# Row sums of a 64 MB tensor: eight blocks of 16 rows a partition in place of three blocks of 32, 48 and 48

## The chip, the core and the metric

The kernel runs on one core of one Trainium2 chip. The time is that of one execution on the device, in microseconds (us). Three runs of the kernel before gave a median of 160.50 us (160.49 to 160.85). A further execution was recorded by the hardware profiler; its views are what is read here.

## The reference

The input `x` has 32 x 512 x 1024 float32 values, 16,384 rows of 1,024 values (4 KB a row, 67.1 MB in all). The output is the sum of each row, 16,384 float32 values (64 KB).

```python
def reference(x):                                   # x: (32, 512, 1024) float32
    return np.sum(x, axis=-1).astype(np.float32)    # (32, 512)
```

## The kernel before, in words

The 16,384 rows are spread over the 128 partitions, 128 rows for each (`C = 128`). They are not given out in one go but in blocks. `BLOCKS = (32, 48, 48)` (L10) says how many consecutive rows of a block belong to one partition: in block 0 partition p has rows 32p to 32p+31, in the second block 48 consecutive rows of those that follow, and so on. The function `block` (L28) makes the two views: `x_b`, with one long line of `n` x 1,024 values a partition, and `out_b`, with `n` results a partition. In memory the first row of one partition is therefore `n` x 4 KB from that of the next: 128 KB in block 0, 192 KB in the others.

Work goes by groups of `G = 16` rows a partition (L42), eight groups in all: two in block 0, three in each other block. A group is 128 x 64 KB = 8.39 MB, loaded into one of three buffers `xt0` to `xt2` (L48). Each partition's 64 KB of a group are one contiguous run.

All transfers are issued by SyncE (the queue "SPq" of the profile), in the order of the list `loads` (L90 to L103, issued at L146 to L149). Group 0 comes as one row (semaphore `first`) and then the 15 others; groups 1 to 6 as one load each; the last group as pieces of 9, 4 and 2 rows (`piece0` to `piece2`, from `CUTS`) and its last row as 544 and 480 values (`tail0`, `tail1`). From the fourth group on SyncE waits, ahead of the load, for VectorE to have reduced the group whose buffer is used again (L148). The two first loads are moved ahead of the start-up of the program (L174 to L194).

VectorE reduces whole groups (L109 to L116); in group 6 ScalarE takes 7 of the 16 rows by activations with an accumulated sum (L132 to L135). The pieces of the last group are shared between both (L118 to L123, L137 to L143), and the last row is reduced by VectorE in two halves (L125 to L129). Each block has its own tile of results, `res0` to `res2`, with a column for each row of a partition.

The end is what the second part of the change touches. After the last load SyncE waits for `piece2` and for the sums of all groups but the last (L150 to L152). It then issues three early stores, one for each block (L153 to L155): 32 columns, 48 columns, and the first 32 of the last block's 48. It waits for every sum (L157, L158), stores the last group's 16 columns (L159), waits for the early stores (L161, L162), clears the semaphores (L163) and waits for the last store (L164).

Of the kernel before, what the change touches and what calls it, by code (L numbers as in the profile page):

```python
# [6 lines left out]
COPY = mybir.ActivationFunctionType.Copy  # L7
X = mybir.AxisListType.X

BLOCKS = (32, 48, 48)  # L10
LEAD = 1
G = 16
BUFS = 3
# [6 lines left out]
def row_sums(nc, x: bass.AP, out: bass.AP):  # L20
# [3 lines left out]
    C = R // P  # L24
    assert R % P == 0 and C == sum(BLOCKS) and all(n % G == 0 for n in BLOCKS)
    out_flat = out.rearrange("a (b c) -> (a b c)", c=1)

    def block(r0, n):  # L28
        x_b = x_flat[r0 : r0 + P * n].rearrange("(p c) d -> p (c d)", p=P)
        out_b = out_flat[r0 : r0 + P * n].rearrange("(p c) -> p c", p=P)  # L30
        return x_b, out_b

    def sbuf(name, n):
        return nc.alloc_sbuf_tensor(name, [P, n], F32)

    n_groups = C // G
    groups, stores = [], []
    r0 = 0
    for k, n in enumerate(BLOCKS):
        x_b, out_b = block(r0, n)  # L40
        res = sbuf(f"res{k}", n)
# [8 lines left out]
    pairs = [sbuf(f"pairs{i}", D // 2) for i in range(3)]  # L50

    names = [f"slot{i}" for i in range(BUFS)] + ["first", "piece0", "piece1", "piece2", "tail0"]
    names += ["tail1", "vec", "act", "early0", "early1", "early2", "store"]
    sems = {n: nc.alloc_semaphore(n) for n in names}
    slots = [sems[f"slot{i}"] for i in range(BUFS)]
    vec, act = sems["vec"], sems["act"]
# [76 lines left out]
    _, res, c = groups[b]  # L133
# [12 lines left out]
    for b, dst, src, s in loads:  # L146
        if b >= BUFS:
            nc.sync.wait_ge(vec, freed[b - BUFS])  # L148
        nc.sync.dma_start(out=dst, in_=src).then_inc(s, 16)  # L149
    nc.sync.wait_ge(sems["piece2"], 16)  # L150
    nc.sync.wait_ge(vec, body_vec)
    nc.sync.wait_ge(act, body_act)  # L152
    for k, (out_b, res, n) in enumerate(stores):  # L153
        m = n - G if k == len(stores) - 1 else n
        nc.sync.dma_start(out=out_b[:, 0:m], in_=res[:, 0:m]).then_inc(sems[f"early{k}"], 16)  # L155
    out_z = stores[-1][0]
    nc.sync.wait_ge(vec, count["vec"])  # L157
    nc.sync.wait_ge(act, count["act"])  # L158
    nc.sync.dma_start(out=out_z[:, c_z : c_z + G], in_=res_z[:, c_z : c_z + G]).then_inc(sems["store"], 16)  # L159

    for k in range(len(stores)):  # L161
        nc.sync.wait_ge(sems[f"early{k}"], 16)  # L162
    nc.sync.sem_clear(range(numbers[0], sems["store"].num))  # L163
    nc.sync.wait_ge(sems["store"], 16).then_inc(sems["store"], -16)  # L164
# [2 lines left out]
def kernel(tc: tile.TileContext, x: bass.AP, out: bass.AP):  # L167
    tc.close()
    tc.compile()  # L169
    nc = tc.nc  # L170
    row_sums(nc, x, out)

    sp = mybir.EngineType.SP
    fn = nc.m.functions[0]
    entry, body = None, None
    for blk in fn.blocks:
        ops = [i for i in blk.instructions if i.engine == sp]
        if entry is None:  # L180
            entry = blk
        elif any(i.opcode == "DMACopy" for i in ops):
            body = blk
            break
    code = list(body.instructions)
    loads = [i for i in code if i.engine == sp and i.opcode == "DMACopy"][:EARLY]
    for load in loads:
        assert not load.sync_info.on_wait
        code.remove(load)
    body.instructions = code  # L190
    code = list(entry.instructions)
    at = next(k for k, i in enumerate(code) if i.engine == sp and i.opcode == "Drain")
    code[at:at] = loads
    entry.instructions = code  # L194
# [29 lines left out]
```

## Time and profile before

| what | value |
|---|---|
| median of three runs | 160.50 us |
| the profiled execution's own time | 160.73 us |
| its span, from the first to the last instruction | 159.4 us |
| VectorE (DVE) busy | 121.5 us |
| ScalarE (ACT) busy | 17.2 us |
| bytes read, written | 67.11 MB, 0.07 MB |
| mean rate over the span | 421 GB/s |
| stores from issue to landing | 1.4 to 1.6 us |

How to read the views: DVE is VectorE, ACT ScalarE, SP (or SPq) SyncE. The row of digits has the busy share of the DMA engines in 40 equal slices of the span, in tenths. The chain that ended last is followed back from the last instruction, at each step to what released it. The timeline has start, duration, engine, line and operation, and in brackets how long the engine had been idle and what ended that. A wait is put down to the one that came last. The table by stretches has, for each stretch, its length, the busy time of VectorE, ScalarE and GpSimd with the number of instructions, the granted clock of TensorE, the share of the DMA engines and the rate.

### The profile page before, as it was taken

How to read it: one execution, taken by the hardware profiler on the slowest of the kernel's cores; microseconds unless marked ns; L12 is line 12 of the kernel's file. 1: busy time of each engine (PE TensorE's matmuls, PEld its weight loads, DVE VectorE, ACT ScalarE, POOL GpSimd, SP SyncE). 2: the span in 40 equal slices, each digit the busy share in tenths (PEclk: the TensorE clock that was granted, in tenths of full speed). 3: DMA queues.
4: the chain of work that ended last, by engine and by line, in shares of the span. 5: the costliest groups of instructions: out<-in, count | busy, mean ns of one | idle time of the engine just before them, and what ended most of it. 6: DMA issues, size and time to landing. Idle time of an engine off the chain costs nothing.

```text
span 159.4 us, 110 instructions
## 1 busy us (share of the span) xinstructions
DVE 121.5 (76%) x17; ACT 17.2 (11%) x31; POOL 0.2 (0%) x4
## 2 busy tenths in 40 slices
DVE  1100059994799968999499994999949999499685
ACT  3000000000000000000000000000000000494694
POOL 0000000000000000000000000000000000000000
DMA  9988996996997989969969969969979799699994
GB/s 378 493 370 370 493 526 263 526 526 263 526 477 312 526 378 411 526 263 526 526 263 526 526 263 526 526 263 526 460 329 526 312 477 526 296 444 444 387 400 151
DMA packets 2448, 67.18 MB, mean 421 GB/s; under 512 B 784, under 2 KB 912, under 8 KB 1168
## 3 DMA queue, kind: packets, MB, share of 16 engines
q1 hardware_dynamic: 2448, 67.18, 98.2%
HBM read 67.11 MB, written 0.07 MB: 421 GB/s over the span
## 4 chain that ended last, share of the span: by engine, by line
DMA 75%; DVE 22%; SPq 1%; issue 0%
DMA xt<-in_x_dram 50%; DMA tail<-in_x_dram 25%; DVE res L63 22%; SPq L149 1%; DVE pairs L81 0%; DVE res L81 0%
## 5 line engine op out<-in xcount | busy, mean ns | idle before, releaser
L63 DVE TENSOR_REDUCE res<-xt 128x16 f32<-128x16384 f32 (+5 forms) x10 | 119.9, 11994 | 34.1 <-DMA xt<-in_x_dram 34.1
L74 ACT ACTIVATE xt<-xt 128x1024 f32<-128x1024 f32 x15 | 15.6, 1043 | 138.3 <-DMA xt<-in_x_dram 138.3
L74 ACT ACTIVATION_READ_ACCUMULATOR xt<-xt 128x1 f32 x15 | 2.8, 187 | 0.0
L107 DVE MEMSET tail<- 128x1 f32 x1 | 0.1, 59 | 2.0 <-PEq L169 2.0
L74 ACT ACT_TABLE_LOAD x1 | 1.3, 1283 | 1.9 <-PEq L169 1.9
L81 DVE CUSTOM_DVE_ANT_0 pairs<-tail 128x272 f32<-128x272 f32 (+1 forms) x2 | 0.9, 428 | 0.1
L81 DVE CUSTOM_DVE_ANT_0 pairs<-xt 128x512 f32<-128x512 f32 x1 | 0.7, 693 | 0.2 <-DMA xt<-in_x_dram 0.2
L81 DVE DVE_READ_ACCUMULATOR2_ANT res<- 128x1 f32 x2 | 0.2, 82 | 0.0
L208 POOL MEMSET const-bfloat16-1.0<- 128x1 bf16 x1 | 0.1, 102 | 0.0
L208 POOL MEMSET const-uint8-127<- 128x1 uint8 x1 | 0.1, 101 | 0.0
L208 POOL MEMSET const-float32-0.0<- 128x1 f32 x1 | 0.1, 99 | 0.2 <-issue 0.2
L208 POOL MEMSET const-float32-1.0<- 128x1 f32 x1 | 0.1, 98 | 0.0
L81 DVE DVE_READ_ACCUMULATOR2_ANT tail<- 128x1 f32 x1 | 0.1, 82 | 0.0
## 6 DMA issues: line engine op xcount, KB each, us to landing
xt<-in_x_dram SPq DMA_DIRECT2D x1, 7680.0 KB, 21.2
xt<-in_x_dram SPq DMA_DIRECT2D x1, 4608.0 KB, 32.6
xt<-in_x_dram SPq DMA_DIRECT2D x1, 2048.0 KB, 37.0
xt<-in_x_dram SPq DMA_DIRECT2D x1, 1024.0 KB, 39.0
xt<-in_x_dram SPq DMA_DIRECT2D x1, 512.0 KB, 3.5
tail<-in_x_dram SPq DMA_DIRECT2D x1, 272.0 KB, 39.2
tail<-in_x_dram SPq DMA_DIRECT2D x1, 240.0 KB, 39.3
xt<-in_x_dram SPq DMA_DIRECT2D x6, 40.8
```

The lines of the kernel that those rows point to most:

```text
L63: nc.vector.tensor_reduce(out=res[:, c : c + n], in_=t[:, j * D : (j + n) * D].rearrange("p (j d) -> p j d", d=D), axis=X, op=ADD,).then_i ...
L74: nc.scalar.activation(out=v, in_=v, func=COPY, accum_out=res[:, c + i : c + i + 1]).then_inc(act, 1)
L81: nc.vector.tensor_tensor_reduce(out=pairs[:, 0 : h - a], in0=t[:, a:h], in1=t[:, h:b], scale=1.0, scalar=0.0, op0=ADD, op1=ADD, accum_out ...
L107: nc.vector.memset(tail[:, CUT + 15 : CUT + 16], 0.0).then_inc(vec, 1)
L149: nc.sync.dma_start(out=dst, in_=src).then_inc(s, 16)
L208: nc = _bacc.Bacc("TRN2", target_bir_lowering=False, num_devices=1)
```

## The change

All blocks become 16 rows a partition, so that every block is one group: a partition's 64 KB are followed directly by the next partition's, and a group is 8 MB of `x` without a gap. The groups, their order, their sizes, the buffers, the pieces and the work of VectorE and ScalarE stay. There are eight result tiles of 16 columns instead of three of 32, 48 and 48. The early stores are one for each of the first seven blocks, 16 columns each; the last block has only the last store. They are issued when `piece1` has arrived and no longer when `piece2` has. The semaphores of the early stores are seven instead of three.

```diff
-BLOCKS = (32, 48, 48)
+BLOCKS = (16,) * 8
...
-    names += ["tail1", "vec", "act", "early0", "early1", "early2", "store"]
+    names += ["tail1", "vec", "act"]
+    names += [f"early{k}" for k in range(len(BLOCKS) - 1)] + ["store"]
...
-    nc.sync.wait_ge(sems["piece2"], 16)
+    nc.sync.wait_ge(sems["piece1"], 16)
     nc.sync.wait_ge(vec, body_vec)
     nc.sync.wait_ge(act, body_act)
-    for k, (out_b, res, n) in enumerate(stores):
-        m = n - G if k == len(stores) - 1 else n
-        nc.sync.dma_start(out=out_b[:, 0:m], in_=res[:, 0:m]).then_inc(sems[f"early{k}"], 16)
+    early = stores[:-1]
+    for k, (out_b, res, n) in enumerate(early):
+        nc.sync.dma_start(out=out_b[:, :], in_=res[:, :]).then_inc(sems[f"early{k}"], 16)
     out_z = stores[-1][0]
...
-    for k in range(len(stores)):
+    for k in range(len(early)):
         nc.sync.wait_ge(sems[f"early{k}"], 16)
```

## The prediction

> **What bounds the kernel now.** I read first the page's busy times, slices and queue, to see which resource is never idle.
>
> ```profile
> span 159.4 us, 110 instructions
> DVE 121.5 (76%) x17; ACT 17.2 (11%) x31; POOL 0.2 (0%) x4
> DMA  9988996996997989969969969969979799699994
> q1 hardware_dynamic: 2448, 67.18, 98.2%
> HBM read 67.11 MB, written 0.07 MB: 421 GB/s over the span
> ```
>
> VectorE is busy for 76% of the span, but the one queue that carries all transfers has its packets on the 16 DMA engines for 98.2% of it. The input alone is 67.11 MB. So the kernel is a stream of loads, and everything else matters only at its two ends. The chain that ended last says the same, in order of time (start, length, what):
>
> ```profile
> 1.91 39.07 DMA xt<-in_x_dram
> 41.00 17.23 DVE res L63
> 58.25 40.78 DMA xt<-in_x_dram
> 118.14 39.32 DMA tail<-in_x_dram
> 157.51 0.41 DVE pairs L81
> ```
>
> The VectorE pieces in this chain are not a bound: a reduction of 17.23 us frees a buffer, and the load then issued takes 40.78 us to land because two others lie ahead of it in the queue, which is therefore never empty. What sets the pace is how long one 8.39 MB load takes. I cut the span at the moments when the reductions of successive groups start (length, VectorE busy, ..., GB/s last):
>
> ```profile
> 21.64:41.00 19.36, 16.15 (x1) 0.00 (x0) 0.00 (x0) 1.00 1.00 433
> 41.00:60.36 19.36, 17.23 (x2) 0.00 (x0) 0.00 (x0) 1.00 1.00 433
> 118.42:137.87 19.45, 17.22 (x1) 0.00 (x0) 0.00 (x0) 1.00 0.94 408
> ```
>
> The first is a load from block 0, whose rows a partition lie 128 KB apart from the next partition's (32 rows of 4 KB). The second is from block 1, 192 KB apart. Both take 19.36 us, 433 GB/s with a DMA share of 1.00. The third ran longest, 19.45 us. (Its 408 GB/s counts a shorter stretch of packets; the length is what I use.) Then the end: the timeline, SyncE's own waits, and the stores' times from issue to landing.
>
> ```profile
> 148.88 4.42 DVE L63 TENSOR_REDUCE res<-xt 128x4 f32<-128x4096 f32 x1 [1.25 <-DMA xt<-in_x_dram]
> 153.74 2.29 DVE L63 TENSOR_REDUCE res<-xt 128x2 f32<-128x2048 f32 x1 [0.44 <-DMA xt<-in_x_dram]
> 156.22 1.30 SPq L155 DMA_DIRECT2D out_dram<-res  x3
> 157.84 0.08 DVE L81 DVE_READ_ACCUMULATOR2_ANT res<- 128x1 f32 x1
> 157.95 0.33 SPq L159 DMA_DIRECT2D out_dram<-res  x1
> ```
>
> ```profile
> SPq L155 <- DMA xt<-in_x_dram: 8.5, 1, 8.5
> SPq L164 <- SPq L164: 0.6, 1, 0.6
> SPq L162 <- DMA out_dram<-res: 0.4, 1, 0.4
> SPq L159 <- DVE res L81: 0.3, 1, 0.3
> ```
>
> ```profile
> out_dram<-res SPq DMA_DIRECT2D x2, 16.0 KB, 1.5
> out_dram<-res SPq DMA_DIRECT2D x1, 24.0 KB, 1.6
> out_dram<-res SPq DMA_DIRECT2D x1, 8.0 KB, 1.4
> ```
>
> The reader is to see that SyncE has three early stores out by about 157.6, waits 0.3 us for the last sum (157.92), issues the last store at 157.95, and that this store's landing, 1.4 us later, ends the span at 159.4. The early stores (L162) hold it 0.4 us, inside those 1.4.
>
> **The change, part by part.** The profiled execution took 160.73 us, its span 159.4, so 1.33 us lie around the span; it is 0.23 above the median of 160.50. The terms below are differences, and I put their sum on the median.
>
> *Loads.* The same 13 loads of the same sizes stay, in the same order, on the same queue and in the same buffers; only their addresses move. Each partition's run stays 64 KB, and the next partition's run begins 64 KB further on instead of 128 or 192. Cost from the nearest rows: going from 192 to 128 KB changes the interval by 19.36 - 19.36 = 0.00 us, so I take 0 for going on to 64. Bound from below (a gain): what a perfect layout could remove. The first 0.52 MB load lands at 3.5 us. The trace's packet records start its first packet at 1.0 us, 0.52 MB at 433 GB/s are 1.2, and a semaphore is seen 0.35 us after its packet: 3.5 - 1.0 - 1.2 - 0.35 = 0.95 us lost. The last 16 rows in five loads take 157.46 - 137.87 = 19.59 us against 19.36, 0.23 lost, and the 19.45 us interval adds 0.09. Together 1.27 us; steady loads have nothing to give. Bound from above: the longest interval on all eight groups gives 8 x (19.45 - 19.36) = 0.7 us; the 9-row piece, 148.88 - 137.87 = 11.01 us for 4.72 MB against 10.89 at the steady pace, is 1.1% longer, and 1.1% of the 156 us stream is 1.7 us. So -1.27 to +1.7, and I take 0, from the pitch row, which is the only one that differs in what is changed.
>
> Here the Trainium skill has a rule, "HBM row pitch at large powers of two" (DMA: Bandwidth & Descriptors, section Latency and other measured facts): copies lost rate as the pitch of the rows grew, 207 GB/s at 512 KiB against 214 in full and 103 at 4 MiB, and it advises contiguous tiles or an odd pitch. If its 3% held for the old pitches too, the change would be worth an estimated 4.7 us; the trace does not agree, since 128 KB, a power of two, and 192 KB both run at 433 GB/s, and the sum stays with that row.
>
> *Seven early stores instead of three.* Removed: three issues after the second-last piece of rows (156.22), 1.30 us on SyncE. Added: seven after the piece before it (153.74). The records put the three starts at 156.22, 156.61 and 157.09, and the last end at 157.57, so one store costs SyncE 0.48 us at most. Seven from 153.74 end at 153.74 + 7 x 0.48 = 157.1. SyncE next needs to be free at 157.92, so 0.8 us of cover remain and the cost on the path is 0. SyncE's other two waits before them are over: the last body reduction ended at 147.62, ScalarE's rows at 145.3. Nothing else is queued behind SyncE then; all loads were issued by 118.6. The wait that is dropped, on the 2-row piece, is contained in the later one for the last sum.
>
> *The seven stores on the DMA engines.* They go to the queue behind the last three loads. Their packets: a 64-byte one took 8 to 11 ns and a semaphore 9, so one store is 8 x 10.4 + 9 = 0.09 us on each engine, seven 0.65. The last load's packets end at 157.12. Six stores are waiting by then, the seventh comes about 0.85 us after its issue, at 157.5; all seven are through by about 157.8. The last store's packets ran at 158.78 to 158.99. Cover 0.9 us, cost 0. If all seven went ahead of the last loads instead, it would be +0.65.
>
> *Queue depth.* At 118.6 six loads were unfinished in the queue; now up to eight transfers are. No row shows eight. If only six fit, the last three stores wait for the loads ending at 155.82, 156.50 and 157.12, and the seventh issue ends near 157.6: still under 157.92, cost 0.
>
> *The last store.* 16 columns as before, but its 64-byte pieces now lie next to each other instead of 192 bytes apart. Rows: 1.4 us to landing for it, 1.5 and 1.6 for the early ones, whose pieces also touch. So 0 to +0.2; I take 0, since it is the only 64-byte row and the others were issued back to back.
>
> *Waits at the end.* Seven waits on early stores, not three, and four more numbers in one clearing instruction (51 ns). They run between 158.3 and the landing at 159.36; the early stores have landed by about 158.2. Seven at about 0.05 us are 0.35: hidden, 0.
>
> Sum: 0 + 0 + 0 + 0 + 0 = 0. Time 160.5 us.
>
> The Trainium skill speaks against many small transfers: about 2.0 us fixed for each, mostly overhead under 64 KB (DMA: Bandwidth & Descriptors, Anatomy of one DMA, and Rules for kernel authors). Taken one after the other, four more would be an estimated 8 us; the trace has three in flight at once 0.4 to 0.5 us apart, so this doesn't bear on the sum.
>
> **Rivals.**
> 1. *The new addresses cost the stream time (slower).* All 16 engines now read runs that start at multiples of 64 KB close together; if that loads the memory unevenly, every group takes longer. For it: packets of loads are now and then late (intervals 19.33 to 19.45), so the memory is not wholly out of the picture. Against it: halving-like steps of pitch (192 to 128) cost nothing. Between 0.7 and 1.7 us by the rows above: 161.2 to 162.2. It decides from 0.48 / 8 = 0.06 us an interval on.
> 2. *The early stores get in front of the last loads (slower).* +0.65: 161.2. Against it: the five last loads, queued together at 118, landed strictly in order, which speaks for a queue served in order. It decides only if five of seven pass.
> 3. *The contiguous loads gain at the ends (faster).* Half of the 1.27 us lost at the start and the end: 159.9. For it: the first load runs well under the steady rate. Against it: that may be mere start-up, the same for any address.
> 4. *Nothing of either part reaches the end* is the forecast itself: loads at a rate that addresses don't touch, stores covered.
>
> **How the numbers follow.** About 0.3% of 160.5, 0.48 us, is what can be told from no change. Forecast 0.50 (160.1 to 160.9); rival 1 0.20; rival 2 0.07; rival 3 0.23. So faster 0.23, same 0.50, slower 0.27. The predicted time is the forecast's, 160.5. For 8 in 10 the range goes to 159.7 below (two thirds of what rival 3 could win) and 161.9 above (most of rival 1's span, all of rival 2).
>
> **What would show it.** Right: intervals between group reductions of 19.36 as before, seven store issues on SyncE from 153.7 to about 157, no wait of SyncE on an early store after the last issue, and the last store still issued about 0.03 us after the last sum and landing 1.4 us later. Wrong by rival 1: intervals above 19.42 in every group. Wrong by rival 2: equal intervals up to 118 but the last two loads landing 0.3 to 0.65 us later after the piece that releases the stores. Wrong by rival 3: the first reduction starting before 3.5, or the 19.59 us of the last group shrinking. A landing of the last store over 1.6 us, or an issue of it that waits for SyncE and not for the last sum, would break the zero of the stores.

## The result, and the profile after

The changed kernel takes 161.36 us (median of 6 runs, 161.18 to 161.78), against 160.65 us (160.49 to 160.86) for the kernel before in the same comparison: a ratio of 1.0043, with a 95% interval of 1.0031 to 1.0055. It is slower by 0.7 us. The prediction was 160.5 us with "same" as the likeliest; the measured time is inside its range, but the interval lies above 1. That is a small loss, but one that can be told from no change, and no change was forecast.

The profiled execution of the changed kernel took 161.18 us, the fastest of its six, and the one of before 160.73, so the two traces differ by 0.45 us and not by 0.7. What the slower executions lose beyond that is in neither trace. Line numbers of the changed kernel are one higher (L63 is now L64).

The page of the changed kernel, on the queue:

```profile
q1 hardware_dynamic: 3024, 67.18, 98.2%
```

Still one queue that is full for 98.2% of the span; the 576 additional packets (2448 before) are those of the small stores. The table by stretches of the changed kernel, again cut where the group reductions start (length first, GB/s last):

```profile
22.26:41.61 19.35, 16.15 (x2) 0.00 (x0) 0.00 (x0) 1.00 1.00 434
41.61:60.95 19.34, 17.22 (x1) 0.00 (x0) 0.00 (x0) 1.00 1.00 434
119.01:138.36 19.35, 17.22 (x1) 0.00 (x0) 0.00 (x0) 1.00 0.95 410
```

These are the intervals that took 19.36, 19.36 and 19.45 us before. The pitch is the distance in memory from one partition's run to the next partition's. In this trace the running stream at a pitch of 64 KB is not slower than before. Its start is what differs. Timeline of the changed kernel, VectorE's first two reductions and the last ones, and the stores:

```profile
3.72 1.22 DVE L64 TENSOR_REDUCE res<-xt 128x1 f32<-128x1024 f32 x1 [1.67 <-DMA xt<-in_x_dram]
22.26 16.15 DVE L64 TENSOR_REDUCE res<-xt 128x15 f32<-128x15360 f32 x1 [17.32 <-DMA xt<-in_x_dram]
...
154.17 3.20 SPq L156 DMA_DIRECT2D out_dram<-res  x7
154.18 2.29 DVE L64 TENSOR_REDUCE res<-xt 128x2 f32<-128x2048 f32 x1 [0.45 <-DMA xt<-in_x_dram]
156.66 0.69 DVE L82 CUSTOM_DVE_ANT_0 pairs<-xt 128x512 f32<-128x512 f32 x1 [0.20 <-DMA xt<-in_x_dram]
157.97 0.41 DVE L82 CUSTOM_DVE_ANT_0 pairs<-tail 128x241 f32<-128x241 f32 x1 [0.17 <-DMA tail<-in_x_dram]
158.30 0.08 DVE L82 DVE_READ_ACCUMULATOR2_ANT res<- 128x1 f32 x1
158.41 0.33 SPq L160 DMA_DIRECT2D out_dram<-res  x1
```

The same two first reductions before:

```profile
3.53 1.22 DVE L63 TENSOR_REDUCE res<-xt 128x1 f32<-128x1024 f32 x1 [1.50 <-DMA xt<-in_x_dram]
21.64 16.15 DVE L63 TENSOR_REDUCE res<-xt 128x15 f32<-128x15360 f32 x1 [16.89 <-DMA xt<-in_x_dram]
```

The first reduction starts at 3.72 us (before: 3.53), the second, of the 15 other rows of group 0, at 22.26 (before: 21.64). So 0.62 us are lost by then: 0.19 in the first row, 0.43 in the 15 rows. The 0.19 can't be put down to the pitch: in the traces of this case that start at 128 KB or more, the first row is reduced at anything from 3.48 to 3.90 us. After that nothing more is lost: group 7 starts 0.49 us late (138.36 against 137.87), the last store is issued 0.46 late (158.41 against 157.95) and lands 1.4 us later, as before. SyncE's own waits of the changed kernel:

```profile
SPq L156 <- DMA xt<-in_x_dram: 6.0, 1, 6.0
SPq L160 <- DVE res L82: 0.5, 1, 0.5
SPq L159 <- ACT xt L75: 0.5, 1, 0.5
```

SyncE issues the seven stores in 3.20 us, from 154.17 to 157.37. Until the last store at 158.41 it then waits about 1.0 us, half of it for ScalarE's last row (L159) and half for VectorE's last sum (L160): the stores are covered. The waits for early stores are still there, though none is in this list: the trace has three instructions for them (L163), started at 158.84, 159.01 and 159.18 as early stores land, after 0.10 to 0.14 us of waiting each. The last store lands after that, at 159.82, so they cost nothing, and nor did the 0.4 us before.

### The profile page after: what moved, and what is told of

It reads as the page before. It is cut to its first block, busy times and chain, and to the rows that moved or that the text cites. A ratio compares the mean times of both kernels' runs of the same rounds, so it can differ in the third digit from the quotient of the medians.

```text
span 159.9 us, 116 instructions
## 1 busy us (share of the span) xinstructions
DVE 121.5 (76%) x17; ACT 17.2 (11%) x31; POOL 0.2 (0%) x4
## 3 DMA queue, kind: packets, MB, share of 16 engines
q1 hardware_dynamic: 3024, 67.18, 98.2%
## 4 chain that ended last, share of the span: by engine, by line
DMA 75%; DVE 22%; SPq 1%; issue 0%
DMA xt<-in_x_dram 50%; DMA tail<-in_x_dram 25%; DVE res L64 22%; SPq L150 1%; DVE pairs L82 0%; DVE res L82 0%
## 5 line engine op out<-in xcount | busy, mean ns | idle before, releaser
L64 DVE TENSOR_REDUCE res<-xt 128x16 f32<-128x16384 f32 (+5 forms) x10 | 119.9, 11993 | 34.5 <-DMA xt<-in_x_dram 34.5
```

What stands on the lines that cost most here:

```text
L64: nc.vector.tensor_reduce(out=res[:, c : c + n], in_=t[:, j * D : (j + n) * D].rearrange("p (j d) -> p j d", d=D), axis=X, op=ADD,).then_i ...
```

## The experiments

Run times are medians; times read from a timeline are those of one profiled execution. The kernels come in three sets, each run on a chip of its own together with the kernel before; a ratio is always to the kernel before of the same set. In the code, "..." stands for lines left out.

**The stores alone.** Blocks as before, stores as changed. This and the next three kernels tell apart the loads' addresses and the stores.

```diff
 BLOCKS = (32, 48, 48)
...
-    nc.sync.wait_ge(sems["piece2"], 16)
+    nc.sync.wait_ge(sems["piece1"], 16)
...
-    for k, (out_b, res, n) in enumerate(stores):
-        m = n - G if k == len(stores) - 1 else n
-        nc.sync.dma_start(out=out_b[:, 0:m], in_=res[:, 0:m]).then_inc(sems[f"early{k}"], 16)
+    early = [(o, r, c, c + G) for o, r, n in stores for c in range(0, n, G)][:-1]
+    for k, (out_b, res, i, j) in enumerate(early):
+        nc.sync.dma_start(out=out_b[:, i:j], in_=res[:, i:j]).then_inc(sems[f"early{k}"], 16)
...
```

> Blocks of 32, 48 and 48 rows as before; seven early stores of 16 columns, issued after the 4-row piece. Theory A (the start of the first block at 64 KB costs it all; stores cost nothing): 160.65 us, ratio 1.000, group 0 reduced from about 21.6 us on. Theory B (the seven stores cost the time, through the queue or SyncE): 161.2 to 161.4, with the last store landing or being issued late.

Measured: 160.88 us against 160.86, ratio 0.9998 (0.9987 to 1.0009). Seven early stores, one piece sooner, cost and bring nothing.

**The pitch of the first groups against that of the others.** From the changed kernel, other blocks (one early store for each block or part of it that is not the last group):

```diff
-BLOCKS = (16,) * 8
+BLOCKS = (16, 16, 48, 48)      # the first; the second (32,) + (16,) * 6, the third (48,) + (16,) * 5
...
```

> Blocks of 16, 16, 48 and 48 rows: groups 0 and 1 lie at 64 KB a partition as in the changed kernel, groups 2 to 7 at 192 KB as before; four early stores. Theory A: as slow as the changed kernel, 161.2 to 161.5 us, group 0 reduced from about 22.2 us on. Rival C (the pitch of all eight groups costs a little each, and the late start in the profile was chance): a quarter of the loss, 160.8. Theory B: 160.65 to 160.8.

> Blocks of 32 and then six of 16 rows: groups 0 and 1 lie at 128 KB as before, groups 2 to 7 at 64 KB as in the changed kernel; six early stores. Theory A: no loss, and if the shorter intervals of the changed kernel (19.34 against 19.37 us) belong to the 64 KB pitch, a gain of 0.1 to 0.2: 160.4 to 160.65 us, group 0 from 21.6 us on. Rival C: three quarters of the loss, 161.2. Theory B: 161.2.

> Blocks of 48 and then five of 16 rows: groups 0 to 2 lie at 192 KB, the others at 64 KB; five early stores. Theory A with the reading that only 64 KB is bad at the start: 160.4 to 160.65 us, group 0 from about 21.6 us on. Theory A with the reading that the start worsens with any smaller pitch: earlier than with 128 KB, group 0 from 21.3 us on, 160.2 us. Rival C: 161.1.

Measured, against 160.86: with 16, 16, 48, 48 it is 161.47 us, ratio 1.0033 (1.0023 to 1.0043). With 32 first 160.93, 1.0004 (0.9992 to 1.0016). With 48 first 160.88, 1.0000 (0.9989 to 1.0012). Two groups of 64 KB pitch at the start bring nearly the whole loss; five or six of them later on bring none that can be told. That is Theory A; Theory B and Rival C had 160.8 or less for the first and 161.1 to 161.2 for the others. Its side reading, that the evener intervals at 64 KB are a gain, is not borne out, and nor is a faster start at 192 KB. In the traces group 0 is reduced from 22.51, 22.03 and 21.91 us on. That the second is later than expected lies in its first row (3.90); its 15 rows take 18.13 us after that, as before (18.11).

How the loss arises shows in single packets, which the views only sum up. Each of the 16 engines moves the 15 rows of group 0 in eight packets of 60 KB, one for each of its eight partitions, one after the other. From the packet records of each trace, the mean of 16 packets by turn, in ns (the shortest is 2,265); some of the rows are from kernels that come further on:

```
                                turn 1     2     3     4     5     6     7     8
before             (128 KB)       2316  2293  2280  2268  2269  2269  2268  2269
stores alone       (128 KB)       2275  2268  2269  2268  2269  2269  2267  2268
32 first           (128 KB)       2268  2268  2268  2268  2269  2269  2267  2269
48 first           (192 KB)       2269  2269  2269  2283  2280  2270  2270  2270
64 and 64          (256 KB)       2273  2270  2270  2268  2270  2277  2305  2303
one block          (512 KB)       2441  2356  2268  2268  2271  2270  2267  2269
changed            ( 64 KB)       2333  2318  2366  2416  2287  2268  2267  2267
16, 16, 48, 48     ( 64 KB)       2278  2268  2286  2348  2280  2267  2267  2267
changed, row 15 first (64 KB)     2309  2332  2376  2384  2302  2267  2267  2267
changed, groups swapped (64 KB)   2625  2324  2332  2332  2271  2267  2267  2267
```

At 64 KB the packets of turns 1 to 5, until about 14 us, are long, most of all those of turn 4; from turn 6 on they are at the floor, their shortest time, and in the changed kernel they stay there (the 64 KB packets of groups 1 to 6 have a mean of 2,419 ns with a shortest of 2,418; before the mean was 2,425). Beyond a floor of 2,267 the eight packets cost 0.39 us an engine in the changed kernel and 0.10 before. One reservation: in the profiled execution with 16, 16, 48, 48 the long packets fell on engines that were ahead, and its late start is mostly its first row (4.39 us) and only a little the 15 others:

```profile
4.39 1.22 DVE L64 TENSOR_REDUCE res<-xt 128x1 f32<-128x1024 f32 x1 [2.35 <-DMA xt<-in_x_dram]
22.51 16.15 DVE L64 TENSOR_REDUCE res<-xt 128x15 f32<-128x15360 f32 x1 [16.90 <-DMA xt<-in_x_dram]
```

The reader is to see two places where time can be lost at the start: the first row (before: 3.53) and the 15 rows after it, which took 22.51 - 4.39 = 18.12 us here, 18.11 before and 18.54 in the changed kernel. Whether the late first row of this execution belongs to the pitch is not shown. For the 15 rows all traces with the 1 and 15 cut, also those further on, can be laid side by side: 18.11 to 18.16 us in the five that start at 128, 192 or 256 KB, 18.34 to 18.80 in four of the five that start at 64 KB, and 18.44 at 512 KB.

**What in the start matters: the cut, the offset, the place in the tensor?** Four kernels, run together. In the first, group 0 is loaded uncut; the second loads row 15 first, so that the 15 others begin at the run's start; the third reads group 1 before group 0; the fourth is the kernel before with group 0 uncut.

```diff
-LEAD = 1
+LEAD = 0
-    loads = [(0, xt[0][:, 0:D], x_0[:, 0:D], sems["first"])]
-    loads.append((0, xt[0][:, D : G * D], x_0[:, D : G * D], slots[0]))
+    loads = [(0, xt[0][:, :], x_0[:, 0 : G * D], slots[0])]
...
```

```diff
+    e = (G - LEAD) * D
+    loads = [(0, xt[0][:, e : G * D], x_0[:, e : G * D], sems["first"])]
+    loads.append((0, xt[0][:, 0:e], x_0[:, 0:e], slots[0]))
...
```

```diff
+    groups[0], groups[1] = groups[1], groups[0]
     x_z, res_z, c_z = groups[-1]
```

> Changed kernel, group 0 as one load of 64 KB a partition and not 4 + 60 KB. Theory A1 (16 streams that start together at 64 KB a partition get in each other's way, until delays have set them apart; whatever the sizes): still slow, 161.2 to 161.6 us, long packets in the first 14 us. Theory A2 (it is the split: runs of 60 KB that begin 4 KB off, at a pitch of 64 KB): back at 160.6 to 160.9.

> Changed kernel, the single first row is row 15 of group 0 and the 15 others begin at the run's start. A1: 161.2 to 161.6 us. A2 with the reading that the 4 KB offset matters: 160.6 to 160.9; with the reading that 60 KB runs matter: 161.3.

> Changed kernel with the first two groups in the other order, so the stream begins 8 MB further into x. A1 and A2: 161.2 to 161.6 us, the loss stays at the start of the stream. Theory A3 (the first 8 MB of the tensor are themselves slow when read densely): the long packets move to the second load, from 22 us on.

> Kernel before (blocks 32, 48, 48, three early stores), group 0 as one load. Control for the run of the changed kernel without the split: A1 and A2 say that at 128 KB the split hardly matters, 160.5 to 160.9 us. If starting small costs time at any pitch, 160.2 to 160.4, which would be faster than both kernels.

Measured, against 160.76: row 15 first 161.31 us, ratio 1.0035 (1.0021 to 1.0048); groups swapped 161.28, 1.0033 (1.0023 to 1.0044). The loss is bound neither to the 4 KB offset nor to a place in the tensor; it stays at the start of the stream. The first reductions of the kernel with the groups swapped:

```profile
3.73 1.22 DVE L65 TENSOR_REDUCE res<-xt 128x1 f32<-128x1024 f32 x1 [1.68 <-DMA xt<-in_x_dram]
22.53 16.15 DVE L65 TENSOR_REDUCE res<-xt 128x15 f32<-128x15360 f32 x1 [17.58 <-DMA xt<-in_x_dram]
41.89 17.22 DVE L65 TENSOR_REDUCE res<-xt 128x16 f32<-128x16384 f32 x1 [3.21 <-DMA xt<-in_x_dram]
```

The second reduction starts at 22.53 and the third 19.36 us later: the long packets did not move to the second load, which now reads the first 8 MB.

The uncut group gave 161.11, 1.0019 (1.0006 to 1.0032), with runs from 160.81 to 161.51: between the expectations. Its trace, of its slowest run, shows no loss at the start but one later on:

```profile
21.90 17.22 DVE L64 TENSOR_REDUCE res<-xt 128x16 f32<-128x16384 f32 x1 [20.34 <-DMA xt<-in_x_dram]
...
79.93 17.22 DVE L64 TENSOR_REDUCE res<-xt 128x16 f32<-128x16384 f32 x1 [2.13 <-DMA xt<-in_x_dram]
99.33 17.22 DVE L64 TENSOR_REDUCE res<-xt 128x16 f32<-128x16384 f32 x1 [2.18 <-DMA xt<-in_x_dram]
118.98 17.22 DVE L64 TENSOR_REDUCE res<-xt 128x16 f32<-128x16384 f32 x1 [2.44 <-DMA xt<-in_x_dram]
```

Group 0 is there at 21.90 (22.26 in the changed kernel, 21.86 in the kernel before without the cut), but 79.93 to 99.33 is 19.40 us and 99.33 to 118.98 is 19.65. So in this execution the start is free of the loss without the cut, and time is lost in mid-stream instead. The kernel with 32 first shows such a stretch too, in its slowest run, which is the profiled one (161.60 us). The kernel before without the cut: 160.79, 1.0002 (0.9991 to 1.0013); at 128 KB the cut is worth nothing either way, and no version here beats both kernels.

**Another cut, two larger pitches, and the stores issued late.** The changed kernel with group 0 cut into 8 and 8 rows (`LEAD = 8` in both places); blocks of 64 and 64 rows, and one of 128, with two and one early stores; and the changed kernel with the old wait ahead of its stores.

```diff
-    nc.sync.wait_ge(sems["piece1"], 16)
+    nc.sync.wait_ge(sems["piece2"], 16)
     nc.sync.wait_ge(vec, body_vec)
```

> Changed kernel, group 0 cut into 8 and 8 rows a partition and not 1 and 15. If the loss at 64 KB comes from a short first load, after which all 16 engines go on almost in step: 160.7 to 161.0 us, as good as the uncut group. If any cut that makes each run of the second load begin away from the end of the run before it does it: 161.2 to 161.5.

> Blocks of 64 and 64 rows: every group at a pitch of 256 KB, two early stores. If only 64 KB is bad: 160.6 to 160.9 us. If the steady rate falls with any power of two above 128 KB: every interval over 19.4 us and the time over 161.2.

> One block of 128 rows: every group at a pitch of 512 KB, one early store. If only 64 KB is bad: 160.6 to 160.9 us. By the Trainium skill (DMA: Bandwidth & Descriptors, Latency and other measured facts), 3% below full rate at 512 KiB, an estimated 165 us, in intervals of 19.9.

> Changed kernel with the seven stores issued after the 2-row piece, as the three were before. The prediction's arithmetic: the piece lands at 156.64, seven stores take 3.2 us, so SyncE is free at 159.84 and not at 157.84, and the last store is issued at 159.9 and not at 158.41: 1.4 to 1.5 us more than the changed kernel, 162.8 us. If SyncE's issues did not hold the last store up: 161.36 as the changed kernel.

Measured, against 160.68: cut in halves 161.28 us, 1.0026 (1.0010 to 1.0042), but with runs from 160.77 to 161.58. Its trace, of a run of 160.92 us, has packets at the floor from the start of the second load on (1,213 ns against a shortest of 1,211). Its median has the second expectation's size, but four of its twelve runs are at 160.95 or less, and the one of them that was traced has no loss at the start. So with another cut the start need not lose time; where the slower runs lose theirs was not traced. With the 1 and 15 cut no run is spared: the lowest of all runs with a 64 KB start and that cut are 161.18 (changed), 161.20 (16, 16, 48, 48), 161.13 (row 15 first) and 161.14 (groups swapped).

At 256 KB 160.99 us, 1.0017 (0.9999 to 1.0034), runs from 160.60 to 161.47; at 512 KB 161.14, 1.0021 (1.0008 to 1.0035). A loss of 0.2% at 512 KB, not 3%, but a loss: that only 64 KB is bad is not borne out. The traces show where, at 512 KB (first fence) and at 256 KB (second):

```profile
3.58 1.22 DVE L64 TENSOR_REDUCE res<-xt 128x1 f32<-128x1024 f32 x1 [1.53 <-DMA xt<-in_x_dram]
22.02 16.15 DVE L64 TENSOR_REDUCE res<-xt 128x15 f32<-128x15360 f32 x1 [17.23 <-DMA xt<-in_x_dram]
```

```profile
99.11 17.22 DVE L64 TENSOR_REDUCE res<-xt 128x16 f32<-128x16384 f32 x1 [2.17 <-DMA xt<-in_x_dram]
118.71 17.22 DVE L64 TENSOR_REDUCE res<-xt 128x16 f32<-128x16384 f32 x1 [2.38 <-DMA xt<-in_x_dram]
```

At 512 KB the 15 rows take 18.44 us, and the first two packets of each engine are long (table above), nearly as in the changed kernel; the intervals after that are 19.34 to 19.40. At 256 KB the start is as before, but 118.71 - 99.11 = 19.60 us, a stretch in mid-stream like the two at 64 KB.

The stores issued late: 162.73 us, 1.0117 (1.0089 to 1.0144), 1.4 us over the changed kernel, as the arithmetic had it. Timeline of that kernel, SyncE's stores:

```profile
156.63 3.20 SPq L156 DMA_DIRECT2D out_dram<-res  x7
159.93 0.38 SPq L160 DMA_DIRECT2D out_dram<-res  x1
```

Its last sum was there at 158.36 (the chain's end, 158.35 + 0.01). The last store waits 1.57 us for SyncE, where in the changed kernel SyncE waits for the sum. The stores start 156.63 - 154.17 = 2.46 us later than in the changed kernel; the 1.04 us that SyncE waited there take up a part of that, and 1.42 are left, which is the loss of 1.4 us. So it is the issue one piece sooner that pays for the four more stores.

## Why the prediction was wrong, point by point

- *What bounds the kernel* was right: one queue, full nearly all the time, and the last store's issue tied to the last landing. A delay of 0.6 us in group 0 came out as 0.5 at the end.
- *Seven early stores: 0.* Right. The forecast had 7 x 0.48 us = 3.36; they took 3.20 and left SyncE 1.04 us of wait (forecast: 0.8). The kernel with the stores alone gives 0.9998, and the one with the late issue shows what the earlier issue was worth, 1.4 us.
- *The seven stores on the DMA engines: 0, and rival 2.* Right, and rival 2 falls: from the 2-row piece to the last half row it took 157.97 - 156.66 = 1.31 us, against 1.28 before. The first store's packets begin at 156.90, 2.7 us after its issue (before: 157.06, 0.84 us after), so the stores waited behind the loads.
- *Queue depth, the last store, the waits at the end: 0.* Right on the path. One size was off: the early stores were to have landed by 158.2, and the last did at 159.17, in time by 0.65 us before the last store at 159.82. It was the landing that was off and not the engines' work: the packets of all seven are through at 158.07 (forecast 157.8), and the last landing is seen 1.1 us after that, where 0.37 us lie between the two for the last store (159.45 and 159.82). So the sign that SyncE waits for no early store after the last issue did not hold, and the zero held all the same. The line with the sum has five zeros for six parts; all six are 0.
- *Loads: 0.* This is the step that failed. It took "going from 192 to 128 KB changes the interval by 0.00 us" as the row for going on to 64 (which is the first halving; from 192 to 128 is a third less). That row was read in the running stream, and of the running stream the forecast was right: 19.34 to 19.35 us at 64 KB. But the start was never compared between pitches, because the kernel before has only one first group, at 128 KB. The loss sits there: when the stream sets out at 64 KB, the packets of the first 14 us run long (0.39 us an engine beyond the floor, 0.10 before), and the 15 rows of group 0 are reduced 0.62 us late. At the end 0.46 us of it is left in the traces, and the medians differ by 0.7. The bound above, +0.7 us, had the right size from the wrong place, by luck.
- *Rival 1*, new addresses that cost time, was the right direction and its lower price, 161.2, the nearest, also by luck. Its mechanism, longer intervals in every group, is refuted by the intervals; its condition (0.06 us more an interval) was not met by a single one. *Rival 3* read the lossy start as something to win with contiguous loads; the contiguous loads made just this start worse.
- *The Trainium skill's rule* "HBM row pitch at large powers of two" (DMA: Bandwidth & Descriptors, Latency and other measured facts), by which copies between tensors in memory run 3% below full rate at a pitch of 512 KiB, and which advises contiguous tiles or a pitch padded by a few KiB, does not carry over to these loads. 512 KB costs 0.2% here (1.0021), and its trace has the loss in the start and not in the rate; the contiguous layout has the highest ratio of the pitches tried with the 1 and 15 cut, 1.0043. No run here has a pitch padded by a few KiB.
- *The 2.0 us for each transfer* that the prediction quotes from the Trainium skill (DMA: Bandwidth & Descriptors, Anatomy of one DMA) is given there for transfers that GpSimd issues. Here SyncE issues them, and the prediction was right to leave it out of the sum: seven stores were issued in 3.20 us and overlapped.

What the runs show is that the loss belongs to the pitch of the first groups, appears while the stream starts, and with another cut of the first group is not there in every execution. That 16 engines which set out at 64 KB a partition hold each other up until they have been set apart, and then run evenly, is an inference from the packet times; no view shows where in the memory they would meet. Left open too are why a start at 512 KB also loses time and one at 256 KB does not, and the losses in mid-stream in some executions, at 64 KB (uncut, 32 first) and at 256 KB.

## What to carry to other kernels

A rate read in mid-stream need not hold at the start of the stream: when addresses change, compare the first load separately, at its own pitch and cut, before writing 0. Contiguous loads were no gain here, where the queue already ran at 433 GB/s. When small stores are added before the end, count their issues against the time until the last sum; here, issuing them one landing sooner hid 3.2 us of issues at no cost.

## What the runs showed of the hardware that was not expected

- Loads of runs with no gap between partitions can be slower at the start than loads with gaps: 161.47 us with two such groups first, 160.88 to 160.93 with 48 or 32 rows first. A gap does not always help: at a pitch of 512 KB the traced start loses time too, 18.44 us for the 15 rows against 18.11.
- After a start at 64 KB with the 1 and 15 cut, the stream ran very evenly: 64 KB packets with a mean of 2,419 to 2,421 ns in the five traces, against 2,425 before. This is not the pitch itself: with 16, 16, 48, 48, where 192 KB follow, the mean is 2,420, and with 32 first, where 64 KB follow, 2,437. One of the five still loses time at the end: with row 15 first the 9-row piece takes 149.62 - 138.33 = 11.29 us, against 10.95 in the changed kernel.
- Adjacent 64-byte stores issued up to 0.48 us apart but held up behind loads land 0.17 to 0.19 us apart (158.12, 158.31, 158.48, 158.66, 158.83, 159.00, 159.17), so their landing time is 3.0 us in the median and not 1.5:

```profile
out_dram<-res SPq DMA_DIRECT2D x8, 8.0 KB, 3.0
```

That line is from the changed kernel's list of DMA issues; in the kernel with the late issue, whose stores find the queue empty, the same line has 1.5.
